# Product-key expert mixer: v tiles of two expert blocks by four feature blocks, and G read four blocks at a time

## The chip, the cores and the metric

The kernel runs on one core of a Trainium2 chip. The metric is the device time of one execution in microseconds (us), the median of several runs. A profiled execution also leaves a trace: for each instruction its engine, its start and its duration, and for idle time before an instruction what released it. The engines are TensorE (PE in the rows; its weight loads are PEld), VectorE (DVE), ScalarE (ACT), GpSimd (POOL) and SyncE (SP, which here only issues transfers).

## What is computed

Two layers of an encoder trunk work on 576 tokens (64 of a running stream and 512 of a new one). Each layer has a token mixer (gated linear attention beside a state-space branch) and then an expert mixer of 16384 experts. Only the expert mixer matters here. Cut to its core:

```python
def one_block(xb):                       # some tokens
    q = (xb @ wq).reshape(n, 8, 256)
    s1, s2 = scores of both halves of q against keys1, keys2      # 128 sub-keys each
    ...                                  # top 16 of each, top 16 of their sums: eidx, gsm = softmax
    u_sel = u_tab[eidx]
    v_sel = v_tab[eidx]
    act = jnp.einsum('td,thkd->thk', xb, u_sel)
    w = gsm * jax.nn.gelu(act, approximate=False)
    return jnp.einsum('thk,thkd->td', w, v_sel)
```

The result, scaled by a modulation vector, is added to the residual, and a norm over the features follows.

## The kernel before

For 448 of the 576 tokens (TD) the expert mixer isn't computed by looking experts up but densely: the weights of all 16384 experts are multiplied. With experts in 128 blocks (EB) of 128, the activations gelu(u x) of one block are a tile of 128 experts by 448 tokens; G, the softmax weights scattered to the same layout (zero where an expert isn't chosen), is multiplied in; and v of the block, 128 experts by 1024 features (8 feature blocks), is multiplied from the left and summed over all blocks. The other 128 tokens (GT) take the way of the reference: 128 rows of u for each token are gathered, one row per token at a time, then 128 rows of v (`gather_u`, `gather_v`; one gather is an indirect transfer issued by GpSimd, its product and sum are one VectorE instruction into `hold`, which lies in two banks of PSUM). At the end the gathered sum is copied to SBUF and transposed by TensorE in eight pieces.

Matrix products are kept near fp32 by splitting each operand in a high and a low part (fp32r): high by a copy on ScalarE, low by a subtraction on GpSimd (for weights) or VectorE (for the expert weights `wh`, `wl`), and three products, high x high, high x low, low x high. So each block of 128x128 costs three matmuls of 448 columns.

The expert mixer runs in this order in `peer()`. First TensorE computes the activations of blocks 0 to 61 (AH) while VectorE does the top-k and G is built; the activations go to DRAM (`a_dram`) and G too (`g_dram`, 7 groups of 64 tokens; in a row of it, 64 tokens of block 0, then of block 1, and so on). Then comes `dense()`, the stage that the change is about. Before, it goes through a list of items, `v_plan`: item i is one feature block d and the expert blocks b0 to b1. An item has eight expert blocks, except for the first seven, which have 1 to 7, and the last eight, which have 8 to 1. For every item one tile of v is loaded (up to 512 KB; the run in DRAM is 128 features, 512 bytes), split, and used for 3 x 8 matmuls into one sum. Sums take turns in the first half of the PSUM tile `work` and a bank of the pool `pa` (four banks, which are also used for the activations `u` and the copies `w`). VectorE then adds the sum to `acc` in SBUF (the first time it copies).

Each step of the list also makes the weights of one block, LW = 2 steps ahead: `weight(b)` reads G for the block (`load_g`, two blocks in a tile, three tiles), reads the stored activation (`load_a`) and copies it to a bank of PSUM on ScalarE, or, for blocks 62 and up, has TensorE compute it just before (`u_mm`, 24 matmuls, then gelu in place). Three further instructions are put on a list and taken from it by `stage()` between the matmuls: the product with G on VectorE (`mul`), the high part on ScalarE (`high`) and the low part on VectorE (`low`).

All instructions of an engine run in the order in which the program issues them. The order on the queues therefore follows the text of the loop. Weight tiles pass through the class `Weights`: raw loads on SP's queue into three buffers (two more in this stage), up to five tiles ahead of the splits; splits two tiles ahead of use. `W.get` issues them. The gathers are driven by the loop itself: every `yield` of `dense()` adds to a counter, and when it passes one the next step of the gathers is issued, so that 264 steps fit in the stage; 259 are used, the last with the transposes. The expert weights have GB + LW = 10 buffers for each part.

Towards the end `residual(d)` reads the residual of a feature block and adds it on VectorE, and `combine(d)` adds a last sum to it, scaled by the modulation. With the last sum of a feature block come the squares for the norm: a square on ScalarE, an add on VectorE (`SumSq.more`), and a product with a matrix of ones on TensorE (`SumSq.mm`), which for blocks 6 and 7 is issued in between.

Of the kernel before, what the change touches and what calls it, by code (L numbers as in the profile page):

```python
# [9 lines left out]
F32 = mybir.dt.float32  # L10
# [8 lines left out]
P = 128  # L19
# [10 lines left out]
EB = 128  # L30
# [3 lines left out]
TG = 64  # L34
NG = TD // TG
GB = 8
LW = 2
AH = 62
RU = 1.7
GC = 0.55  # L40
G0 = 4
# [138 lines left out]
def hybrid_kernel(ctx, tc, A, O):  # L180
# [16 lines left out]
    def pat(name):  # L197
        return pa.tile([P, 512], F32, name=name, tag="pa")
# [880 lines left out]
    def v_plan():  # L1079

        out = [(d, 0, d) for d in range(1, GB)]
        out += [(n % GB, n, n + GB) for n in range(EB - GB)]
        return out + [(d, EB - GB + d, EB) for d in range(GB)]

    def peer(l, h2, h2t, nxt, pq):
        hh, hl = h2
# [3 lines left out]
        ub, vb = {}, {}  # L1092
        for i in range(AH):
            ub[i] = W.add([A["uT"][l, i]])
        for i, (d, b0, b1) in enumerate(plan):
            if AH <= i + LW < EB:
                ub[i + LW] = W.add([A["uT"][l, i + LW]])
            vb[i] = W.add([A["v"][l, b0:b1, :, d * P:(d + 1) * P].rearrange("b e c -> e b c")], vpl, "v")
        W.stop = vb[0]
        if l + 1 < L:  # L1100
            add_mixer(l + 1)
# [48 lines left out]
        def gather_v():  # L1150
            AC.activation(act, act, AF.Gelu)
            DV.tensor_mul(gw, gw, act)
            for j in range(P):
                g = gp.tile([P, D], F32, name=f"gv{j}", tag="g")
                PO.indirect_dma_start(out=g, out_offset=None, in_=A["v"].rearrange("l b e d -> (l b e) d"),  # L1155
                                      in_offset=bass.IndirectOffsetOnAxis(ap=gidx[:, j:j + 1], axis=0))
                if j >= 3:
                    vadd(j - 3)
                gts[j] = g
                yield 1  # L1160
            for j in range(P - 3, P):
                vadd(j)
            yield 1
            xg = gp.tile([P, KB, GT], F32, name="xg", tag="g")
            nc.sync.dma_start(xg, xs_dram[:, :, TD:T])
            gacc = gp.tile([P, D], F32, name="gacc", tag="g")
            AC.activation(gacc, hold, AF.Copy)
            yield 1
            for i in range(2):
                ps = pat(f"gt{l}_{i}")  # L1170
                for b in range(4):
                    PE.transpose(ps[:, b * P:(b + 1) * P], gacc[:, (4 * i + b) * P:(4 * i + b + 1) * P], ident)
                for b in range(4):
# [258 lines left out]

        def load_g(b):

            if b % 2 == 0 and b < EB:
                t_ = dp.tile([P, NG, 2 * TG], F32, name=f"gt{b}", tag="gt", bufs=3)
                nc.sync.dma_start(
                    t_, g_dram[l].rearrange("g p c -> p g c")[:, :, b * TG:(b + 2) * TG])
                gtile[b] = gtile[b + 1] = t_

        def load_a(b):
            if b < AH:
# [5 lines left out]

        def weight(b):

            load_g(b + 4)
            load_a(b + 3)
            if b < AH:
                ps = pat(f"w{l}_{b}")
                AC.activation(ps[:, :TD], ag.pop(b), AF.Copy)
            else:
                ps = ups.pop(b)
                AC.activation(ps[:, :TD], ps[:, :TD], AF.Gelu)  # L1458
            wh = dp.tile([P, TD], F32R, name=f"wh{b}", tag="wh", bufs=GB + LW)
            wl = dp.tile([P, TD], F32R, name=f"wl{b}", tag="wl", bufs=GB + LW)  # L1460

            def mul():
                pv = ps[:, :TD].rearrange("p (g t) -> p g t", t=TG)
                o = b % 2 * TG
                DV.tensor_tensor(pv, pv, gtile.pop(b)[:, :, o:o + TG], op=ALU.mult)

            def high():
                AC.activation(wh, ps[:, :TD], AF.Copy)

            def low():  # L1470
                DV.tensor_tensor(wl, ps[:, :TD], wh.bitcast(F32), op=ALU.subtract)  # L1471
                ws[b] = (wh, wl)

            stages.extend([mul, high, low])

        def stage(n=1):
            for _ in range(n):
                if stages:
                    stages.pop(0)()

        def dense():

            for b in (0, 2):
                load_g(b)
            for b in range(3):
                load_a(b)
            for b in range(LW):
                weight(b)
                stage(3)
            first = set()  # L1490
            for i, (d, b0, b1) in enumerate(plan):
                b = i + LW
                if AH <= b < EB:
                    for _ in u_mm(b):
                        yield 6 * RU
                    yield 6 * RU
                if b < EB:
                    weight(b)
                if b0 == EB - GB:
                    for _ in gat:  # L1500
                        pass
                vh, vl = W.get(vb[i])
                ps = (pat(f"vo{l}_{i}") if i % 2 else work[:, 0, :])[:, :TD]
                n = b1 - b0
                for k in range(n):
                    wh, wl = ws[b0 + k]
                    ds_ = slice(k * P, (k + 1) * P)
                    for j, (vv_, ww) in enumerate(((vh, wh), (vh, wl), (vl, wh))):
                        PE.matmul(ps, vv_[:, ds_], ww, start=k == 0 and j == 0, stop=k == n - 1 and j == 2)  # L1509
                    if k % 2 == 1 and k < n - 1:  # L1510
                        stage()
                        yield 6
                stage(3)
                if b0 >= EB - 2 * GB:
                    combine(d, ps, b1 == EB)
                elif d not in first:
                    first.add(d)
                    DV.tensor_copy(acc[:, d, :TD], ps)
                else:
                    DV.tensor_tensor(acc[:, d, :TD], acc[:, d, :TD], ps, op=ALU.add)  # L1520
                if EB - 3 * GB <= b0 < EB - 2 * GB:
                    residual(d)
                yield 6

        ga2 = m[:, 40:48, :]
        sq_ = []

# [8 lines left out]
        def combine(b, ps, last):  # L1536
# [2 lines left out]
                                        op0=ALU.mult, op1=ALU.add)  # L1539
            if last:  # L1540
                if not sq_:
                    sq_.append(SumSq(dp, 3, f"xo{l}", "gt", 3))
# [137 lines left out]
```

## Time and profile before

| | us |
|---|---|
| median of 3 runs | 5200.94 (5195.92 to 5211.62) |
| the profiled execution | 5198.86 |
| its span in the trace | 5197.1 |

| engine | busy us | share of the span |
|---|---|---|
| TensorE | 4945.4 | 95% |
| VectorE | 3227.8 | 62% |
| GpSimd | 2898.7 | 56% |
| ScalarE | 1962.7 | 38% |

The mean granted clock of TensorE is 0.977 of full speed. The stage `dense()` lies at about 1680 to 2650 us for layer 0 and 4220 to 5180 us for layer 1, some 37% of the span. In it the transfers are at their densest: 295 to 340 GB/s, against a mean of 180.

The busy time of an engine is what its instructions took; a matmul is pipelined, so that one of 448 columns is shown with 0.36 us although the next begins 0.2 us later. A row of the timeline has the start, the duration, the engine, the line, the operation with its output and inputs, and in brackets how long the engine sat idle before and what released it. A row of the chain of work has the start, the duration and what ran.

### The profile page before, as it was taken

The page shows a single profiled execution, that of the slowest core. Times are in us where ns is not written, and L with a number is a line of the kernel's source. Part 1 is how long each engine was busy: PE and PEld are TensorE (multiplying, and loading weights), DVE is VectorE, ACT ScalarE, POOL GpSimd, SP SyncE. Part 2 cuts the span into 40 slices and gives each one's busy share as a digit, 9 for nine tenths or more (in the row PEclk, how much of TensorE's full clock was granted, in tenths as well). Part 3 has the DMA queues.
Part 4 walks back from the last instruction along what each step waited for, and adds up shares of the span by engine and source line. Part 5 has one row for each costly group of instructions (what it writes and reads, how often), then busy time and mean ns, then how long its engine had stood idle before and what let it go on. Part 6 is the DMA issues. An engine that isn't in the chain of part 4 may idle for free.

```text
span 5197.1 us, 77582 instructions
## 1 busy us (share of the span) xinstructions
PE 4945.4 (95%) x29892; PEld 4558.6 (88%) x29892; DVE 3227.8 (62%) x6513; ACT 1962.7 (38%) x3020; POOL 2898.7 (56%) x1986
## 2 busy tenths in 40 slices
PE   8988999989998999999989889998999999999998
PEld 6977888879888999999889878998998889999997
DVE  4687631359997665555646886414799956655564
ACT  3333332233377443223233332423234854332232
POOL 3356543334444777877743555533344557777875
PEclk9999999999999999999999999999999999999999
DMA  3211246523446998888822111232243589988894
GB/s 141 70 58 53 74 139 203 168 95 109 144 153 229 335 338 296 295 297 302 274 78 70 62 50 54 78 100 96 66 146 123 214 271 340 315 297 297 298 310 157
DMA packets 594897, 934.64 MB, mean 180 GB/s; under 512 B 29889, under 2 KB 443073, under 8 KB 591073
## 3 DMA queue, kind: packets, MB, share of 16 engines
q1 hardware_dynamic: 498032, 563.70, 35.5%
q0 software_dynamic: 73728, 268.47, 13.8%
q10 hardware_dynamic: 22768, 97.52, 4.7%
q8 instruction: 237, 3.88, 0.3%
q14 instruction: 132, 1.07, 0.1%
HBM read 826.53 MB, written 103.04 MB: 179 GB/s over the span
## 4 chain that ended last, share of the span: by engine, by line
PE 57%; DVE 20%; issue 9%; POOL 8%; ACT 4%; DMA 2%; ACTq 0%; POOLq 0%; DVEq 0%; SPq 0%
PE pj L476 23%; PE vo L1509 9%; PE work L1509 9%; PE u L1117 8%; POOL wlo L111 3%; DVE tix L1229 2%; POOL gv L1155 2%; DVE cv L635 2%; DVE tv L1228 2%; DVE teq L1304 1%; DVE teid L1312 1%; DVE teq L1309 1%; DVE ob L1394 1%; ACT stg L1369 1%; DVE s L1231 1%
## 5 line engine op out<-in xcount | busy, mean ns | idle before, releaser
L111 POOL TENSOR_TENSOR wlo<-raw,whi 128x1024 fp32r<-128x1024 f32 (+1 forms) x510 | 1265.4, 2482 | 1640.6 <-ACT whi L110 1606.2
L111 POOL TENSOR_TENSOR vlo<-raw,vhi 128x1024 fp32r<-128x1024 f32 (+3 forms) x270 | 620.9, 2300 | 359.8 <-ACT vhi L110 355.9
L110 ACT ACTIVATE whi<-raw 128x1024 fp32r<-128x1024 f32 (+1 forms) x510 | 538.7, 1056 | 219.1 <-issue 149.3
L1117 PE MATMUL u<-n_0hi,whi 128*128 128x448 f32 x1024 | 383.6, 375 | 9.1 <-DVE tsc L1293 7.0
L1117 PE MATMUL u<-n_1hi,whi 128*128 128x448 f32 x1024 | 383.0, 374 | 9.1 <-DVE tsc L1293 7.0
L1509 PE MATMUL work<-wh,vhi 128*128 128x448 f32 x1024 | 376.2, 367 | 14.0 <-ACT vhi L110 14.0
L1117 PE MATMUL u<-n_0hi,wlo 128*128 128x448 f32 x1024 | 377.9, 369 | 3.5 <-POOL wlo L111 3.5
L1117 PE MATMUL u<-n_1hi,wlo 128*128 128x448 f32 x1024 | 377.7, 369 | 3.3 <-POOL wlo L111 3.3
L1458 ACT ACTIVATE u<-u 128x448 f32<-128x448 f32 x132 | 69.7, 528 | 816.3 <-PE u L1117 806.3
L1117 PE MATMUL u<-n_0lo,whi 128*128 128x448 f32 x1024 | 377.7, 369 | 0.0
L1117 PE MATMUL u<-n_1lo,whi 128*128 128x448 f32 x1024 | 377.2, 368 | 0.0
L1509 PE MATMUL vo<-wh,vlo 128*128 128x448 f32 x1024 | 374.9, 366 | 0.7 <-POOL vlo L111 0.7
L1509 PE MATMUL vo<-wh,vhi 128*128 128x448 f32 x1024 | 375.0, 366 | 0.3 <-DVE wl L1471 0.3
L1509 PE MATMUL work<-wl,vhi 128*128 128x448 f32 x1024 | 375.2, 366 | 0.0
L1509 PE MATMUL work<-wh,vlo 128*128 128x448 f32 x1024 | 374.9, 366 | 0.0
L1509 PE MATMUL vo<-wl,vhi 128*128 128x448 f32 x1024 | 374.8, 366 | 0.0
L1184 DVE SCALAR_TENSOR_TENSOR hold<-gv,gw,hold 128x1024 f32<-128x1024 f32 x254 | 326.4, 1285 | 54.6 <-DMA gv<-in_v,gidx 51.8
L110 ACT ACTIVATE vhi<-raw 128x1024 fp32r<-128x1024 f32 (+3 forms) x270 | 271.8, 1008 | 136.4 <-issue 94.3
L1148 DVE SCALAR_TENSOR_TENSOR gu<-gu,hold 128x1024 f32<-128x1024 f32 x256 | 307.5, 1213 | 16.2 <-DMA gu<-in_u,gidx 16.0
L1394 DVE TENSOR_SCALAR ob<-work,sT 128x128 f32<-128x128 f32 x896 | 295.5, 401 | 0.7 <-PE gb L1368 0.6
L476 PE MATMUL pj<-n_0hi,whi 128*128 128x288 f32 x1248 | 285.6, 311 | 1.4 <-ACT whi L110 1.4
L476 PE MATMUL pj<-n_1hi,whi 128*128 128x288 f32 x1248 | 283.3, 309 | 0.1
(526 smaller groups left out, 12648.9 us busy)
## 6 DMA issues: line engine op xcount, KB each, us to landing
raw<-in_wblk SPq DMA_DIRECT2D x256, 512.0 KB
raw<-in_uT SPq DMA_DIRECT2D x256, 512.0 KB
raw<-in_v SPq DMA_DIRECT2D x242, 512.0 KB
gt<-g_dram SPq DMA_DIRECT2D x128, 448.0 KB
adaw<-in_w_ada SPq DMA_DIRECT2D x96, 512.0 KB
g_dram<-stg ACTq DMA_DIRECT2D x12, 4096.0 KB
a_dram<-ag ACTq DMA_DIRECT2D x124, 224.0 KB
ar<-a_dram SPq DMA_DIRECT2D x124, 224.0 KB
```

The costliest lines, as they stand in the source:

```text
L110: self.nc.scalar.activation(hi, r, AF.Copy)
L111: self.nc.gpsimd.tensor_tensor(lo, r, hi.bitcast(F32), op=ALU.subtract)
L476: PE.matmul(ps[:mcols, a, :HT], w[:, ws], xx[:, k, H2[a]], start=k == 0 and j == 0, stop=k == nk - 1 and j == 2)
L635: DV.scalar_tensor_tensor(c, ext[:, i:i + N], w[:, 4 * cb + i:4 * cb + i + 1], c, op0=ALU.mult, op1=ALU.add)
L1117: PE.matmul(ps[:, :TD], w[:, ws], x[:, k, :TD], start=k == 0 and j == 0, stop=k == KB - 1 and j == 2)
L1148: DV.scalar_tensor_tensor(g, g, 1.0, hold, op0=ALU.mult, op1=ALU.mult, accum_out=act[:, j:j + 1])
L1155: PO.indirect_dma_start(out=g, out_offset=None, in_=A["v"].rearrange("l b e d -> (l b e) d"), in_offset=bass.IndirectOffsetOnAxis(ap=gidx[ ...
L1184: DV.scalar_tensor_tensor(hold, g, gw[:, j:j + 1], hold, op0=ALU.mult, op1=ALU.add)
L1228: DV.max(v[:n, ti, b, js], sb_)
L1229: DV.max_index(ix[:n, ti, b, js], v[:n, ti, b, js], sb_)
L1394: DV.tensor_scalar(ob[:, j, :], iotp, sT[:, 1, tk:tk + 1], sT[:, 2, tk:tk + 1], op0=ALU.is_equal, op1=ALU.mult)
L1509: PE.matmul(ps, vv_[:, ds_], ww, start=k == 0 and j == 0, stop=k == n - 1 and j == 2)
```

## The change

A v tile now holds two expert blocks by four feature blocks (the run in DRAM is 512 features, 2 KB), always 512 KB, so 128 tiles for a layer. Features are in two halves, h = 0 and 1. One tile gives 24 matmuls: six into each of four sums, which lie in the two halves of `work` and in two banks of `pa` that are held for the stage. A sum runs over eight expert blocks, four tiles, then four sums are evicted, and the other half of the features takes the banks. The half h = 1 begins with a short sum over blocks 0 to 3 and ends with one over 124 to 127, so that the halves are offset by four blocks.

LW goes from 2 to 4, and before the loop the four weights are issued before the first of their further steps, of which six are taken there. The expert weights have 8 buffers instead of 10. G is read for four blocks at once (runs of 1 KB, 896 KB a tile), two tiles instead of three. The residual steps are taken one at a time at the beginning of a tile's matmuls, behind `weight(b)`. The transposes of the gathered sum write to `hold2`, the PSUM tile that held it, instead of banks of `pa`. The squares at the end have two buffers instead of three.

```diff
-LW = 2
+LW = 4
+VB = 8
+QF = 4
@@ v_plan
-        out = [(d, 0, d) for d in range(1, GB)]
-        out += [(n % GB, n, n + GB) for n in range(EB - GB)]
-        return out + [(d, EB - GB + d, EB) for d in range(GB)]
+        sums = [(1, 0, GB // 2)]
+        for c in range(0, EB, GB):
+            sums += [(0, c, c + GB), (1, c + GB // 2, min(c + GB // 2 + GB, EB))]
+        return [(h, c, c == c0, c + 2 == c1) for h, c0, c1 in sums for c in range(c0, c1, 2)]
@@ peer
-            vb[i] = W.add([A["v"][l, b0:b1, :, d * P:(d + 1) * P].rearrange("b e c -> e b c")], vpl, "v")
+            vb[i] = W.add([A["v"][l, c:c + 2, :, h * QF * P:(h + 1) * QF * P].rearrange("b e c -> e b c")], vpl, "v")
@@ gather_v
-                ps = pat(f"gt{l}_{i}")
+                ps = hold2[:, i, :]
@@ load_g
-            if b % 2 == 0 and b < EB:
-                t_ = dp.tile([P, NG, 2 * TG], F32, name=f"gt{b}", tag="gt", bufs=3)
+            if b % 4 == 0 and b < EB:
+                t_ = dp.tile([P, NG, 4 * TG], F32, name=f"gt{b}", tag="gt", bufs=2)
...
@@ weight
-            load_g(b + 4)
+            load_g(b + 3)
...
-            wh = dp.tile([P, TD], F32R, name=f"wh{b}", tag="wh", bufs=GB + LW)
+            wh = dp.tile([P, TD], F32R, name=f"wh{b}", tag="wh", bufs=VB)
@@ dense
-            for b in (0, 2):
-                load_g(b)
+            load_g(0)
             for b in range(3):
                 load_a(b)
             for b in range(LW):
                 weight(b)
-                stage(3)
+            stage(6)
...
                 if b < EB:
                     weight(b)
-                if b0 == EB - GB:
+                if res:
+                    residual(res.pop(0))
+                if h == 0 and c == EB - GB:
                     for _ in gat:
                         pass
                 vh, vl = W.get(vb[i])
-                ps = (pat(f"vo{l}_{i}") if i % 2 else work[:, 0, :])[:, :TD]
...
+                for q in range(QF):
+                    d, ps = h * QF + q, accs[q]
+                    for k in range(2):
+                        wh, wl = ws[c + k]
+                        ds_ = slice((k * QF + q) * P, (k * QF + q + 1) * P)
+                        for j, (vv_, ww) in enumerate(((vh, wh), (vh, wl), (vl, wh))):
+                            PE.matmul(ps, vv_[:, ds_], ww, start=begin and k == 0 and j == 0,
+                                      stop=end and k == 1 and j == 2)
+                    stage(3 if q == QF - 1 else 1)
+                    if end:
+                        done = c + 2
+                        if done > (EB - 2 * GB if h == 0 else EB - 3 * GB // 2):
+                            combine(d, ps, done == EB)
...
+                        if done == (EB - 2 * GB if h == 0 else EB - 3 * GB // 2):
+                            res.append(d)
+                    yield 6
+        accs = [work[:, i, :TD] for i in range(2)] + [pat(f"va{l}_{i}")[:, :TD] for i in range(2)]
...
-        whole = sum(3 * (b1 - b0) + 24 * RU * (AH <= i + LW < EB) for i, (d, b0, b1) in enumerate(plan)
-                    if b0 < EB - GB - 2)
+        whole = sum(24 + 24 * RU * (AH <= i + LW < EB) for i in range(len(plan) - 6 - 2))
```

## Rows read from the trace of the kernel before

**Rows 1.** Stretches of 100 us: busy time by engine, PEclk, DMA share, GB/s

```profile
1700.00:1800.00 100.00, 100.00 (x495) 92.67 (x494) 62.36 (x109) 43.06 (x65) 75.18 (x47) 1.00 1.11 339
2300.00:2400.00 100.00, 100.00 (x496) 92.66 (x495) 56.89 (x63) 31.20 (x44) 78.00 (x52) 1.00 0.87 295
```

**Rows 2.** Chain of work in order of time: start, us, what; the ninth item, both layers

```profile
1711.67 4.87 PE work L1509 x24
4251.40 4.86 PE work L1509 x24
```

**Rows 3.** TensorE's waits, 1680 to 2650 us: us in total, times, longest

```profile
PE work L1509 <- ACT vhi L110: 7.1, 2, 6.9
```

**Rows 4.** Timeline at the beginning of dense(): start, duration, engine, line, operation

```profile
1685.99 0.74 PE L1509 MATMUL work<-wh,vhi 128*128 128x448 f32 x1 [6.89 <-ACT vhi L110]
...
4225.41 0.74 PE L1509 MATMUL work<-wh,vhi 128*128 128x448 f32 x1 [6.88 <-ACT vhi L110]
...
4226.32 0.58 PE L1509 MATMUL work<-wh,vlo 128*128 128x448 f32 x1
4226.69 0.58 PE L1509 MATMUL vo<-wh,vhi 128*128 128x448 f32 x1
...
1681.71 0.55 ACT L1455 ACTIVATE w<-ar 128x448 f32<-128x448 f32 x1 [0.60 <-DMA ar<-a_dram]
...
1685.64 1.02 ACT L110 ACTIVATE vhi<-raw 128x128 fp32r<-128x128 f32 x3
...
1703.09 1.04 ACT L110 ACTIVATE vhi<-raw 128x1024 fp32r<-128x1024 f32 x1
...
1683.54 0.62 DVE L1471 TENSOR_TENSOR wl<-w,wh 128x448 fp32r<-128x448 f32 x1 [0.61 <-ACT wh L1468]
...
1704.21 2.42 POOL L111 TENSOR_TENSOR vlo<-raw,vhi 128x1024 fp32r<-128x1024 f32 x1 [2.29 <-ACT vhi L110]
...
1673.78 0.37 SPq L100 DMA_DIRECT2D raw<-in_v  x1
1674.37 0.97 SPq L1437 DMA_DIRECT2D gt<-g_dram  x2
```

**Rows 5.** Stretches of 1 us at the same place, columns as in rows 1

```profile
1679.00:1680.00 1.00, 0.10 (x1) 0.00 (x0) 0.00 (x0) 0.55 (x1) 0.00 (x0) 1.00 1.14 362
...
1681.00:1682.00 1.00, 0.00 (x0) 0.00 (x0) 0.00 (x0) 0.40 (x2) 0.00 (x0) 0.60 1.07 357
...
1691.00:1692.00 1.00, 1.00 (x5) 0.91 (x4) 0.00 (x0) 1.00 (x3) 0.36 (x1) 0.78 1.04 308
```

**Rows 6.** Timeline at the end of the stage, layer 0, VectorE and TensorE

```profile
2637.41 0.81 DVE L1538 SCALAR_TENSOR_TENSOR acc<-vo,mod,acc 128x64 f32<-128x64 f32 x2
...
2639.70 0.80 DVE L1538 SCALAR_TENSOR_TENSOR acc<-work,mod,acc 128x64 f32<-128x64 f32 x2
...
2642.22 1.21 PE L281 MATMUL xo<-xo0q,ones 128*128 128x288 f32 x4 [1.81 <-DVE xo0q L267]
...
2645.71 1.24 PE L281 MATMUL xo<-xo0q,ones 128*128 128x288 f32 x4 [0.70 <-ACT xo0q L260]
```

**Rows 7.** Timeline: the last gather and the transposes of its sum, both layers

```profile
2573.42 0.95 POOL L1155 DMA_INDIRECT gv<-in_v,gidx  x1 [0.16 <-DVE hold L1184]
...
2584.06 1.97 PE L1172 MATMUL gt<-ident,gacc 128*128 128x128 f32 x8 [4.16 <-ACT gacc L1167]
...
5110.31 0.95 POOL L1155 DMA_INDIRECT gv<-in_v,gidx  x1 [0.16 <-issue]
...
5120.63 1.09 PE L1172 MATMUL gt<-ident,gacc 128*128 128x128 f32 x8 [1.00 <-ACT gacc L1167]
```

**Rows 8.** Timeline of VectorE in mid-stage: an eviction, a product with G, a gather product

```profile
1813.85 0.62 DVE L1520 TENSOR_TENSOR acc<-acc,work 128x448 f32<-128x448 f32 x1 [1.85 <-PE work L1509]
1814.39 0.63 DVE L1465 TENSOR_TENSOR w<-w,gt 128x448 f32<-128x448 f32 x1
1814.93 1.21 DVE L1148 SCALAR_TENSOR_TENSOR gu<-gu,hold 128x1024 f32<-128x1024 f32 x1
```

More of the change, by code (lines that the diff above doesn't have):

```diff
@@ L1094, in peer @@
             ub[i] = W.add([A["uT"][l, i]])
-        for i, (d, b0, b1) in enumerate(plan):
+        for i, (h, c, _, _) in enumerate(plan):
             if AH <= i + LW < EB:
                 ub[i + LW] = W.add([A["uT"][l, i + LW]])
-            vb[i] = W.add([A["v"][l, b0:b1, :, d * P:(d + 1) * P].rearrange("b e c -> e b c")], vpl, "v")
+            vb[i] = W.add([A["v"][l, c:c + 2, :, h * QF * P:(h + 1) * QF * P].rearrange("b e c -> e b c")], vpl, "v")
         W.stop = vb[0]
@@ L1433, in load_g @@
         def load_g(b):
-            if b % 2 == 0 and b < EB:
-                t_ = dp.tile([P, NG, 2 * TG], F32, name=f"gt{b}", tag="gt", bufs=3)
+            if b % 4 == 0 and b < EB:
+                t_ = dp.tile([P, NG, 4 * TG], F32, name=f"gt{b}", tag="gt", bufs=2)
                 nc.sync.dma_start(
-                    t_, g_dram[l].rearrange("g p c -> p g c")[:, :, b * TG:(b + 2) * TG])
-                gtile[b] = gtile[b + 1] = t_
+                    t_, g_dram[l].rearrange("g p c -> p g c")[:, :, b * TG:(b + 4) * TG])
+                for i in range(4):
+                    gtile[b + i] = t_
         def load_a(b):
@@ L1458, in weight @@
                 AC.activation(ps[:, :TD], ps[:, :TD], AF.Gelu)
-            wh = dp.tile([P, TD], F32R, name=f"wh{b}", tag="wh", bufs=GB + LW)
-            wl = dp.tile([P, TD], F32R, name=f"wl{b}", tag="wl", bufs=GB + LW)
+            wh = dp.tile([P, TD], F32R, name=f"wh{b}", tag="wh", bufs=VB)
+            wl = dp.tile([P, TD], F32R, name=f"wl{b}", tag="wl", bufs=VB)
             def mul():
                 pv = ps[:, :TD].rearrange("p (g t) -> p g t", t=TG)
-                o = b % 2 * TG
+                o = b % 4 * TG
                 DV.tensor_tensor(pv, pv, gtile.pop(b)[:, :, o:o + TG], op=ALU.mult)
@@ L1488, in dense @@
                 weight(b)
-                stage(3)
-            first = set()
-            for i, (d, b0, b1) in enumerate(plan):
+            stage(6)
+            seen = set()
+            for i, (h, c, begin, end) in enumerate(plan):
                 b = i + LW
@@ L1502, in dense @@
                 vh, vl = W.get(vb[i])
-                ps = (pat(f"vo{l}_{i}") if i % 2 else work[:, 0, :])[:, :TD]
[L1504 to L1523, printed above, removed]
+                for q in range(QF):
[11 more added lines that the diff above has]
+                            combine(d, ps, done == EB)
+                        elif d not in seen:
+                            seen.add(d)
+                            DV.tensor_copy(acc[:, d, :TD], ps)
+                        else:
+                            DV.tensor_tensor(acc[:, d, :TD], acc[:, d, :TD], ps, op=ALU.add)
+                        if done == (EB - 2 * GB if h == 0 else EB - 3 * GB // 2):
+                            res.append(d)
+                    yield 6
+        res = []
+        accs = [work[:, i, :TD] for i in range(2)] + [pat(f"va{l}_{i}")[:, :TD] for i in range(2)]
         ga2 = m[:, 40:48, :]
@@ L1541, in combine @@
                 if not sq_:
-                    sq_.append(SumSq(dp, 3, f"xo{l}", "gt", 3))
+                    sq_.append(SumSq(dp, 3, f"xo{l}", "gt", 2))
                 if b >= 6:
```

## The prediction

> **What bounds the kernel now.** The change touches only the last stage of each layer's expert mixer, dense() and the gathers woven into it. I read the stretches of that stage first. From about 1700 to 2570 us (layer 0) and 4250 to 5110 us (layer 1) TensorE is busy for 100.00 of every 100 us at granted clock 1.00 [rows 1]; the reader is to see that VectorE (57 to 62%) and GpSimd (75 to 78%) are not full, and that the DMA share falls from 1.11 to 0.87 when the stored activations stop, while TensorE does not change. Next the chain in order of time: an item of 24 matmuls takes 4.87 us, 0.203 us each [rows 2]. The number of such matmuls is the same before and after: 1024 blocks x 3 for v and 66 x 24 for u, in each layer. So a faster transfer in mid-stage buys nothing, and the change can win or lose only where TensorE waits: at the stage's beginning (6.9 us before the first v matmul), at the transposes of the gathered sum (4.2 and 1.0 us) and in the last few us [rows 3, 4, 6, 7]. The waits in rows 4, 6 and 7 add up to 20.7 us over both layers, some 23 with the end of layer 1 like that of layer 0, 0.44% of the time; no gain can pass that unless a matmul itself gets cheaper, and no row shows why it should.
>
> **The beginning of the stage.** Before, the first v tiles are short (1, 2, 3 expert blocks), so the loads ahead are 64, 128 and 192 KB, the first three splits on ScalarE take 1.02 us together, and the first low part is small [rows 4]. After, each tile is 512 KB. Let t0 be the start of the first w copy, 1681.71 us in layer 0; it waits for the first stored activation [rows 4].
> - The third raw load is issued at 1673.78, right ahead of the G and activation reads [rows 4]. It grows by 320 KB; at 362 GB/s [rows 5] that is 0.9 us more in front of that activation. The two G tiles of 448 KB become one of 896 KB, the same bytes. Longer rows may give back a part, so between 0 and 0.9 us: I take t0 + 0.5.
> - LW = 4 puts four w copies (0.55 us each) ahead of everything else on ScalarE. The fourth needs three more reads of 224 KB, 1.9 us at 360 GB/s, so they end at t0 + 2.5. The split of two weights goes back and forth between ScalarE and VectorE (0.6 us a step [rows 4]): wh of block 0 to 3.0, wl 3.7, product of block 1 to 4.3, wh of block 1 to 4.9.
> - Then the loop begins with weight(4), whose copy stands on ScalarE ahead of the v splits. Its activation is read behind the next G tile: 896 + 224 KB after t0 + 1.9, 3.2 us, so t0 + 5.1; the copy ends at 5.7 (between 5.5 and 6.5). Queued behind it are three v splits of 1.04 us [rows 4]; TensorE waits for the first: 6.8 us, against 4.28 before (1685.99 less 1681.71).
> - The third matmul needs the low part: 2.42 us on GpSimd [rows 4], so the matmuls flow from t0 + 9.2, 1691.4 us with t0 moved by 0.5.
> - The clock: it was granted 0.60 in 1681 to 1682, and 0.78 in 1691 to 1692, between them the lower level (1.2 GHz), back to 1.00 about 5.5 us after the first v matmul [rows 5]. There a matmul starts every 0.37 us [rows 4]. The same 5.5 us from 1691.4 on give 15 matmuls by 1696.9, and 2 came before.
> - Before, 108 matmuls (items of 1 to 8 blocks) were done at 1711.67 [rows 2]. After: 17 + (1711.67 - 1696.9) / 0.203 = 90. The loss is 18 matmuls, 3.7 us. In layer 1 with 4225.41 for 1685.99 and 4251.40 for 1711.67 [rows 2, 4] it is 16.5 matmuls, 3.3 us. **Together +7.0 us**; bounds +2 (t0 not moved, the w copy not last, the clock back sooner) and +11 (a second late transfer).
> The Trainium skill, DMA: Bandwidth & Descriptors, section Specifications, puts the least transfer for line rate at 512 B, which the rows of the old v tiles already have; by it longer rows would give nothing back, t0 would move by the full 0.9 us and the sum would be 0.8 us higher. The DMA share of 1.07 to 1.14 at 357 to 362 GB/s [rows 5] is with 512 B rows and speaks for it.
>
> **Mid-stage.** Loads, splits (128 full tiles for 135, the same bytes) and evictions (132 for 135) stay hidden under TensorE's 4.87 us for a tile. G reads go from 64 to 32 on SP's queue. What is new is the reuse of a sum. Before, two banks take turns and an eviction has a whole item of 24 matmuls. After, four sums end in one tile, each is evicted when its six matmuls are through, and its bank is needed 18 matmuls, 3.65 us, later (42 matmuls where a u block stands between). On VectorE such a tile has four evictions and two weight steps of 0.62 and one or two gather products of 1.21 [rows 8], 5 to 6 us of work spread over 4.87 + 3.65 us; the first eviction ends some 2 us into the tile, the last 1.5 us after it, each 2 us or more ahead of its bank's reuse. The eviction of the old kernel starts 0.25 us after its matmuls where VectorE is idle [rows 8]. Cost 0; if VectorE is late by more, see the first rival. Two banks are left for u and w where there were four (one of them lent to every second sum): a u bank is free again after the block's last weight step in the same tile, one tile ahead of need.
>
> **The gathers.** The pace constant divides by 5410 instead of 5568 weighted matmuls, so gathers come 2.9% faster: 3.16 instead of 3.07 in a tile with u. TensorE stalls at the transposes because from the last gather's place to theirs there are 48 matmuls, 9.73 us, while the chain (gather, three sums, copy) took 10.64 and 10.3 us, and began late by 3.3 and 0.4 us [rows 7]. The places are again 48 matmuls apart. The residual steps, in which VectorE waits for a transfer, now stand behind the load of the u block rather than behind that of v, so I expect the late start of layer 0 to shrink: 1.5 us of stall in each layer, **-2 us together** (bounds -5.2, both gone, and +4, both as late as 3.3 + 1 with combines in between).
>
> **The end.** Combine, square and add of one feature block take 2.29 us in turn between VectorE and ScalarE [rows 6]. Before, the last sums end 9, 6 and 3 matmuls apart, and the flush of squares before the last three matmuls waits 1.81 us for the chain [rows 6]. After, feature blocks 4 to 7 end 1.22 us apart: block 4 starts in the chain 3.4 us before the nominal end (3 x 1.22 less 0.25), so after two turns of 2.29 the flush begins 1.4 us behind it; then come 1.2 us of flush, six matmuls instead of three, the last combine, square and sum: 7.0 us from the nominal last matmul to the last sum, against 5.9 before (2642.22 - 1.81 + 0.6 = 2641.0 to 2646.95 [rows 6]). **+1.0 us in each layer** (0 to 1.5).
>
> **Sum.** +7.0 - 2.0 + 2.0 = +7 us against the profiled execution, 5198.9 us (span 5197.1 and 1.8 us around it), so 5206. That execution lay 2.1 us under the median of the three runs, so 5208.
>
> **Rivals.**
> - *Late evictions (slower).* VectorE is in order, and in the v-only part it holds gather products that can wait for a transfer. If it is more than 2 us behind at the ends of sums, TensorE stands still at each. The price: 15 sums end in that part of a layer, 30 in all; one gather product of 1.21 us too late at each is 36 us, 5244 us, and the clock may fall in the pauses. It decides from 3.65 us between an eviction's matmuls and its end. Against it speaks the 0.25 us [rows 8].
> - *The loads ahead pay (no loss, or faster).* Three full tiles lie ready (1.5 MB for 0.4), the activations behind them arrive sooner and the beginning costs nothing; with the gather stall gone it gives -3 us or so, 5198. A gain over 15.6 us would need two thirds of all 23 us of waits.
> - *The sums cycle through banks.* If TensorE pauses a little between groups of six in four banks and the clock falls, a matmul costs 0.37 instead of 0.203 us [rows 2, 4]; over a tenth of the two stages (1850 us) that is some 80 us, 5290. Rows 1 show 1.00 with a change of bank at every 24. The Trainium skill, TensorE: Matmul & The Clock Gate, section "A second HAM failure mode: psum-queue depth-cycling", tells of a kernel that lost throughput in this way.
> - *It does not do what it says where it counts:* longer rows lower the DMA share, and no engine gets faster. This is inside the forecast.
>
> **How the numbers follow.** Forecast with its bounds 0.77; late evictions 0.12, mostly over the bound; loads that pay 0.08, half of it within the bound; bank cycling 0.03. A measurement of this kernel tells about 0.3%, 15.6 us, from no change. Faster by more 0.04; within 0.78; slower by more 0.18 (0.11 + 0.03 + 0.04 from the upper end of the forecast). The forecast's own range: +7 with the bounds of its parts taken together gives about -3 to +16, with the spread of the runs 5194 to 5220; with the smaller cases of late evictions 5194 to 5225.
>
> **What would show it.** The first v matmul about 7.3 us after the old t0 instead of 4.28, behind a w copy and a full split, and a wait on the low part after it; 108 matmuls done 3 to 4 us later; mid-stage slices still 100.00 at clock 1.00, with a lower DMA share in the v-only part; transposes waiting 0 to 3 us; the flush of squares waiting longer. Wrong would be waits of TensorE on VectorE at the ends of sums, a mid-stage slice under 99, or a matmul that isn't 0.203 us.

## The result

| | before | after |
|---|---|---|
| device time, median | 5200.2 us | 5336.1 us |
| ratio, 95% interval | | 1.0257 (1.0238 to 1.0277) |
| profiled execution / its span | 5198.9 / 5197.1 us | 5330.8 / 5328.8 us |
| packets of the queue that SP fills / MB / share | 498032 / 563.70 / 35.5% | 242832 / 563.70 / 33.4% |

The changed kernel is slower by 2.6%, some 135 us, where 8 us were forecast and 5225 us was the upper end. The longer rows did halve the packets. TensorE lost time in another place. Stretches of 100 us of the changed kernel, columns as in [rows 1]:

```profile
1700.00:1800.00 100.00, 97.14 (x472) 88.01 (x471) 59.38 (x103) 39.17 (x60) 67.52 (x42) 1.00 0.92 322
2300.00:2400.00 100.00, 97.86 (x481) 89.73 (x480) 58.81 (x65) 28.64 (x40) 78.36 (x53) 1.00 0.87 303
2500.00:2600.00 100.00, 86.70 (x413) 79.47 (x412) 53.54 (x66) 25.15 (x34) 65.63 (x44) 0.93 0.78 266
```

Against [rows 1] TensorE's 100.00 has become 96 to 99 in mid-stage, with 472 and 481 matmuls in 100 us for 495 and 496. The granted clock is 1.00 in all but one of the stretches from 1700 to 2500 us (0.98 from 2100 to 2200 us); from 2500 us on it falls further. TensorE's waits in layer 0 of the changed kernel (us in total, times, longest), to be read against [rows 3]:

```profile
PE work L1514 <- DVE acc L1525: 34.3, 27, 12.6
PE work L1514 <- DVE acc L1545: 14.0, 4, 11.3
PE work L1514 <- ACT vhi L112: 10.6, 1, 10.6
PE work L1514 <- DVE acc L1523: 1.4, 2, 0.7
PE work L1514 <- POOL vlo L113: 1.3, 1, 1.3
PE hold L1175 <- DVE acc L1178: 1.3, 1, 1.3
```

Lines 1523, 1525 and 1545 are the three ways in which a sum leaves its bank. The layer has 33 sets of four sums, and there are 27 + 4 + 2 = 33 waits: one at the end of each set. Layer 1 has the same (34.4, 14.1 and 1.4 us); the two layers make 99.6 us. One such end, as pieces of the chain in order of time, and in the timeline:

```profile
1737.73 1.25 PE work L1514 x6
1738.98 0.02 issue
1739.00 0.63 DVE acc L1525
1739.63 0.04 issue
1739.68 1.50 PE work L1514 x6
1741.18 2.48 PE va L1514 x12
```

```profile
1739.00 0.62 DVE L1525 TENSOR_TENSOR acc<-acc,work 128x448 f32<-128x448 f32 x1 [2.53 <-PE work L1514]
1739.68 0.47 PE L1514 MATMUL work<-wh,vhi 128*128 128x448 f32 x1 [0.71 <-DVE acc L1525]
```

Six matmuls into one half of the tile `work` end; VectorE, idle for 2.53 us, evicts that half at once; TensorE waits for it, and only then come the six matmuls into the other half, which nothing has to be evicted from. Those six take 1.50 us instead of 1.22. So a stop costs 0.71 + 0.28 us even with VectorE ready and waiting. Of the 66 stops 58 are of this kind: 0.7 to 0.9 us each, 42.5 us together, with the eviction begun within 0.25 us of the last matmul. At the other eight, 57.1 us, VectorE is late: four are of 11.3 to 13.0 us and four of 1.0 to 3.3 us.

Where the time went, by the n-th matmul of the stage (all matmuls counted from the first v matmul, in the timelines of before and after; the time of the n-th after less that before):

| part of the stage | layer 0 | layer 1 |
|---|---|---|
| up to the 108th matmul, with what lies ahead of the stage | +2.8 us | +1.5 us (64.2 from 62.7) |
| 108th to 4000th | +32.4 | +35.0 |
| 4000th to 4400th (the residual steps) | +25.4 | +29.2 |
| 4400th to the last, the 4676th (with the squares) | +2.0 | +3.4 |

They add up to 131.7 us, by which the spans differ. The second line is the short stops, in the main: the 27 waits of layer 0 on line 1525 without the longest are 26 in 21.7 us, two of them with a late VectorE (1.6 and 3.0 us); with 0.28 us each for the slow restart, 29.0 us; a slower pace of some matmuls, told of below, adds 2.2. The third line is two long waits, 12.6 and 11.3 us. Around the first of them (timeline):

```profile
2548.40 0.38 SPq L102 DMA_DIRECT2D raw<-in_v  x1
2548.83 0.46 SPq L1440 DMA_DIRECT2D gt<-g_dram  x1
2549.35 0.55 SPq L1538 DMA_DIRECT2D xb<-xs_dram  x1
2558.94 0.82 DVE L1540 SCALAR_TENSOR_TENSOR acc<-acc,mod,xb 128x64 f32<-128x64 f32 x2 [10.34 <-DMA xb<-xs_dram]
2560.20 0.61 DVE L1525 TENSOR_TENSOR acc<-acc,work 128x448 f32<-128x448 f32 x1
2560.87 0.74 PE L1514 MATMUL work<-wh,vhi 128*128 128x448 f32 x1 [12.59 <-DVE acc L1525]
```

The residual's load xb is issued behind a v tile of 512 KB and the new G tile of 896 KB and lands 9.6 us later. VectorE stands at the residual step for 10.34 us, the product and the eviction stand behind it, and TensorE behind the eviction. The same in small, in mid-stage, behind a gather of u (two rows of the timeline, and the 10 us that follow, columns as in [rows 1]):

```profile
2183.89 1.22 DVE L1151 SCALAR_TENSOR_TENSOR gu<-gu,hold 128x1024 f32<-128x1024 f32 x1 [3.39 <-DMA gu<-in_u,gidx]
...
2188.65 0.74 PE L1514 MATMUL work<-wh,vhi 128*128 128x448 f32 x1 [2.97 <-DVE acc L1525]
```

```profile
2190.00:2200.00 10.00, 10.00 (x47) 9.22 (x46) 5.52 (x7) 1.20 (x2) 6.11 (x5) 0.92 0.97 343
```

VectorE waits 3.39 us for the gathered rows, the eviction is late, TensorE stops for 2.97 us, and the granted clock behind the stop is 0.92. Layer 1 has such a stop of 3.26 us, and each layer one more, of 1.6 and 1.0 us.

### The profile page after: what moved, and what is told of

The parts are those of the page before. It is cut to its first block, busy times and chain, and to the rows that moved or that the text cites. A ratio compares the mean times of both kernels' runs of the same rounds, so it can differ in the third digit from the quotient of the medians.

```text
span 5328.8 us, 77248 instructions
## 1 busy us (share of the span) xinstructions
PE 4976.1 (93%) x29892; PEld 4562.3 (86%) x29892; DVE 3224.3 (61%) x6507; ACT 1953.6 (37%) x3006; POOL 2894.9 (54%) x1972
## 3 DMA queue, kind: packets, MB, share of 16 engines
q1 hardware_dynamic: 242832, 563.70, 33.4%
## 4 chain that ended last, share of the span: by engine, by line
PE 64%; DVE 20%; issue 5%; POOL 4%; ACT 4%; DMA 2%; ACTq 0%; SPq 0%; DVEq 0%; POOLq 0%
PE pj L478 22%; PE work L1514 11%; PE u L1120 11%; PE va L1514 11%; DVE tix L1232 2%; POOL wlo L113 2%; DVE cv L637 2%; DVE tv L1231 2%; DVE teq L1307 1%; DVE teid L1315 1%; DVE teq L1312 1%; DVE ob L1397 1%; ACT stg L1372 1%; DVE s L1234 1%; PE gb L1371 1%
## 5 line engine op out<-in xcount | busy, mean ns | idle before, releaser
L113 POOL TENSOR_TENSOR vlo<-raw,vhi 128x1024 fp32r<-128x1024 f32 x256 | 615.1, 2404 | 458.2 <-ACT vhi L112 441.3
L112 ACT ACTIVATE vhi<-raw 128x1024 fp32r<-128x1024 f32 x256 | 269.8, 1055 | 323.3 <-issue 298.9
L1514 PE MATMUL va<-wh,vhi 128*128 128x448 f32 x1024 | 377.9, 369 | 0.0
L1514 PE MATMUL va<-wl,vhi 128*128 128x448 f32 x1024 | 377.0, 368 | 0.0
L1514 PE MATMUL va<-wh,vlo 128*128 128x448 f32 x1024 | 376.4, 368 | 0.0
L1514 PEld LDWEIGHTS work<-wh,vhi 128*128 128x128 f32 x1024 | 194.7, 190 | 161.3 <-DVE acc L1525 89.1
L1469 DVE TENSOR_TENSOR u<-u,gt 128x448 f32<-128x448 f32 x132 | 83.3, 631 | 335.5 <-ACT u L1462 325.3
```

The costliest lines, as they stand in the source:

```text
L112: self.nc.scalar.activation(hi, r, AF.Copy)
L113: self.nc.gpsimd.tensor_tensor(lo, r, hi.bitcast(F32), op=ALU.subtract)
L1514: PE.matmul(ps, vv_[:, ds_], ww, start=begin and k == 0 and j == 0, stop=end and k == 1 and j == 2)
```

## The experiments

Theory A: the two halves of `work` are one tile, and the waits go by the tile, so a matmul into one half waits for the eviction of the other. Theory B, the prediction's first rival: evictions come late, and a bank's own reuse waits. Theory C, its third: filling four banks in turn slows TensorE.

| kernel | median us | ratio to before (interval) | slow-paced matmuls of some 4600, layer 0 / 1 |
|---|---|---|---|
| after | 5336.1 | 1.0257 (1.0238, 1.0277) | 540 / 972 |
| sums interleaved | 5287.8 | 1.0162 (1.0121, 1.0204) | 1074 / 2022 |
| evictions later | 5271.3 | 1.0132 (1.0088, 1.0176) | 3576 / 510 |
| xb ahead | 5291.3 | 1.0171 (1.0129, 1.0212) | 1008 / 1008 |
| interleaved, xb ahead | 5236.2 | 1.0068 (1.0047, 1.0088) | 546 / 3492 |
| the same, v split early | 5252.4 | 1.0092 (1.0058, 1.0126) | 852 / 1344 |
| before, sums in two halves | 5344.9 | 1.0260 (1.0220, 1.0299) | 792 / 654 |
| four mendings | 5239.2 | 1.0060 (1.0036, 1.0083) | 282 / 3486 |
| the same, G two at a time | 5237.2 | 1.0055 (1.0036, 1.0073) | 3954 / 564 |
| three mendings | 5218.0 | 1.0044 (1.0031, 1.0057) | 588 / 3198 |
| the same, lead of three | 5205.0 | 1.0011 (0.9998, 1.0024) | 462 / 402 |
| the same, halves as a pair inside | 5212.1 | 1.0024 (1.0007, 1.0042) | 4278 / 4248 |

The last column counts, in the profiled execution, matmuls in groups of six that ran at 0.2067 instead of 0.2027 us each (by the starts in the timeline, the groups without a stop). Each ratio is against executions of the kernel before in the same session; their medians lie between 5193.6 and 5203.6 us, so versions of different sessions are to be compared by their ratios.

**Sums interleaved.**

```diff
-accs = [work[:, i, :TD] for i in range(2)] + [pat(f"va{l}_{i}")[:, :TD] for i in range(2)]
+va = [pat(f"va{l}_{i}")[:, :TD] for i in range(2)]
+accs = [work[:, 0, :TD], va[0], work[:, 1, :TD], va[1]]
```

> The two halves of the tile `work` are no longer used one behind the other: the order of the four sums is work half 0, va_0, work half 1, va_1. Theory A (the two halves count as one tile, so the six matmuls into half 1 wait for VectorE to have read half 0): the eviction of half 0 gets six matmuls, 1.2 us, of cover; the 31 or so short waits of 0.7 to 0.9 us in each layer go, 25 us a layer, and the two long ones of 11 to 13 us in each layer get 1.2 us shorter: 5336 - 55 = about 5280. Theory B (VectorE is late with the evictions as such, so that a bank's own reuse waits): nothing of that changes, 5336. Theory C (four banks filled in turn slow TensorE down): 5336 as well.

5287.8 us. TensorE's waits on evictions in layer 0:

```profile
PE work L1514 <- DVE acc L1525: 15.5, 6, 11.6
PE work L1514 <- DVE acc L1546: 12.8, 2, 12.0
```

Of 33 waits 8 are left, two of them the long ones. With the same four banks, the same evictions and the same work on VectorE, 25 stops are gone because six matmuls into another tile stand between the halves. That is A; B and C expected nothing.

**Evictions one group later.** Each sum is evicted behind the next group's six matmuls, the last two together.

```diff
-if end:
+for d, ps in ([(h * QF + q - 1, accs[q - 1])] * (q > 0) + [(d, ps)] * (q == QF - 1)) if end else []:
```

> Order of the sums as in the changed kernel, but the eviction of each sum is issued one group of six matmuls later (the last two together), so no matmul of the same tile follows an eviction of the other half of `work`, except in the next tile. Theory A: the short waits go as in the interleaved kernel, though every eviction is later; the long waits in the residual stretch fall by up to 2.4 us: about 5275. Theory B: later evictions make the reuse wait longer, 5340 to 5380. Theory C: 5336.

5271.3 us. A later eviction is better, which B rules out. The waits of layer 0:

```profile
PE work L1514 <- ACT vhi L112: 17.7, 2, 10.4
PE hold L1175 <- ACT gacc L1170: 10.5, 1, 10.5
PE work L1514 <- DVE acc L1525: 2.2, 4, 0.6
```

The long waits at sums are gone as well, but VectorE still waits for xb, and the delay comes out at a v split ahead of the transposes (7.3 of the 17.7 us; the other 10.4 are the stage's beginning) and at the transposes (10.5).

**The residual's load ahead.** In the changed kernel, each xb is loaded in the tile in which its sum ends, one to four tiles before its use.

```diff
+load_x(d)
 res.append(d)
...
-t_ = dp.tile([P, TD], F32, name=f"xb{b}", tag="ag", bufs=4)
-nc.sync.dma_start(t_, xs_dram[:, b, :TD])
+t_ = xbs.pop(b)
```

> Only the loads of the residual are moved: each is issued in the tile in which its sum ended, one to four tiles ahead of the residual steps that use it; the residual steps stay at the tile's start. Theory A with the residual as amplifier: VectorE no longer waits 9 to 10 us for the load at the two tiles where a sum ends, so the waits of 12.6 and 11.3 us in each layer fall to under 1 us, 45 us together, with some us for the clock that fell in them: 5336 - 50 = about 5286; the short waits stay, 27 or so a layer. Rival (the long waits have another cause, the gathers or the raw loads): 5330 to 5340.

5291.3 us, 45 less. The waits of layer 0; line 1551 is combine, 1545 in the changed kernel:

```profile
PE work L1514 <- DVE acc L1525: 22.5, 27, 3.3
PE work L1514 <- DVE acc L1551: 3.6, 4, 0.9
```

All stops are still there, and the longest is 3.3 us: the load made the two long ones out of ordinary ones. The 3.3 us are the stop behind the gather. At the transposes TensorE now waits 5.0 us, for 1.3 in the changed kernel.

**Both.**

> Sums in the order work half 0, va_0, work half 1, va_1, and the residual's loads ahead. If the two causes are all there is beside the stage's beginning and end (about +11 us) and some matmuls at 0.207 us (about 5 us): 5336 - 55 - 50 less what is shared = 5215 (5205 to 5230). If something else in the change costs (full v tiles, four G blocks at a time, two banks less for u and w), it stays above 5240.

5236.2 us: 48 + 45 us of the two alone should give 5243, so they do not overlap. But some 35 us over the kernel before stayed, above the range expected. At a sum's end the chain now shows this:

```profile
1734.29 0.62 DVE acc L1525
1734.91 1.14 DVE gu L1151 x2
1736.05 0.54 DVE wl L1475
1736.58 0.54 DVE acc L1525
1737.25 1.45 PE work L1514 x6
```

Here the first rival is seen by itself, in small: two gather products and a weight step stand between two evictions, and TensorE waits, 6 times and 4.1 us in layer 0.

**The first v blocks split early**, added to both: fetched and split after two w copies instead of five.

```diff
-for b in range(LW):
+for b in range(2):
     weight(b)
+got = W.get(vb[0])
+for b in range(2, LW):
+    weight(b)
```

> Sums interleaved and the residual's loads ahead as in the kernel with both (5236 us), and the first v blocks are fetched and split behind the second w copy instead of behind the fifth. Theory (the beginning's cost is the order on ScalarE: five w copies ahead of the first v split): TensorE's wait for the first high part falls from 10.4 to about 6.5 us in each layer, 8 us together: 5228. Rival (the bytes of three full v tiles ahead of the activations cost it, so the order doesn't matter): 5236. Uncertain by some 10 us, because stretches of matmuls at 0.207 us come and go from run to run.

5252.4 us: not faster. The theory of ScalarE's order falls. TensorE's first wait only changes its cause (8.7 us for wh instead of 10.4 for vhi), and the activation read now stands on SP behind the v tiles. The kernel with four mendings, below, has the same beginning; its chain there:

```profile
1693.26 10.19 DMA ar<-a_dram
...
1706.73 1.49 PE work L1519 x3
```

A read of 224 KB takes 10.19 us from issue, and TensorE stands 4.86 us at the first sum's end. From the first v matmul to the 54th, the two profiles with this order lose 6 to 7 us in each layer against the kernel before; with the change's own order, in the kernels with both and with three mendings, it is 0.8 to 1.3 us. The chain points to the bytes ahead of the activations, of which this order puts more there; no run moves them alone.

**The kernel before with its two sums in the two halves of `work`**, nothing else changed.

```diff
-ps = (pat(f"vo{l}_{i}") if i % 2 else work[:, 0, :])[:, :TD]
+ps = work[:, i % 2, :TD]
```

> The kernel before with one line changed: its two sums that take turns lie in the two halves of the tile `work`, where one of them had a tile of its own. Nothing of the change itself is in it. Theory A (two halves of one PSUM tile count as one for the waits): TensorE stops at each of the 264 ends of items until VectorE has read the other half, 0.8 to 1.2 us each: 5200 + 264 x 1.0 = 5465 (5410 to 5520). Theory B (late evictions, or the new order of sums, or four banks in turn): a bank is reused as before, 5200.

5344.9 us: one line makes the old kernel as slow as the changed one. The size was over-estimated, since I counted all 264 ends: where a u block stands between two items its 24 matmuls cover the eviction. The chain, and two stretches of 100 us:

```profile
1734.32 5.11 PE work L1509 x24
1739.45 0.63 DVE acc L1520
1740.22 5.21 PE work L1509 x24
```

```profile
1700.00:1800.00 100.00, 85.75 (x400) 73.88 (x401) 50.83 (x89) 35.37 (x52) 59.15 (x37) 1.00 0.87 277
2300.00:2400.00 100.00, 100.00 (x495) 92.70 (x494) 57.91 (x62) 28.84 (x40) 79.87 (x54) 1.00 0.88 298
```

From one item to the next it is 5.9 us instead of 4.87 [rows 2], and with u blocks between, 100.00 again. No v tile, order of sums or G tile of the change is in this kernel. Theory A is shown. By the trace it is the end of VectorE's eviction that releases TensorE; whether a program must have this wait between two banks of one tile is not tested.

**Four mendings**: evictions later, xb ahead, early v split, and the transposes of both halves of hold2 ahead of VectorE's reading of the first (they had the same wait, 1.3 us).

> The changed kernel with four mendings: each eviction issued one group of six matmuls later, the residual's loads ahead, the first v split behind the second w copy, and the transposes of both halves of hold2 ahead of VectorE's reading of the first. If stalls of TensorE, and the slower pace of 0.207 us that follows some of them, are all that the change cost, what is left is the order of the end: 5200 (5190 to 5215), level with the kernel before or a little faster. If the full v tiles or the four G blocks cost anything by themselves, it stays over 5220.

**The same with G two blocks at a time** (`load_g`, and the buffers of the squares, as before).

> The same with G read back two expert blocks at a time, as in the kernel before (64 reads of 448 KB in place of 32 of 896 KB). By the prediction the size of the G reads is worth nothing, as they lie under TensorE's work: within 10 us of the kernel with all mendings. If the larger G reads help (fewer issues on SP's queue) it is slower by more; if they hurt (the raw loads behind them come late) it is faster by more.

5239.2 and 5237.2 us. The first is far above the 5200 expected, and the size of the G reads is not the reason: undone, it changes nothing. What was left had to be the beginning, which the early split had made worse, and the pace (3768 matmuls at 0.004 us, 15 us, in the profile of the first).

**Three mendings**: without the early split.

> The changed kernel with three of the four mendings: evictions one group of six matmuls later, the residual's loads ahead, both transposes ahead of VectorE's reading; the beginning of the stage is left as the change has it. Theory (the other order at the beginning cost 7.5 us in each layer up to the 54th v matmul, by the two profiles with it): 5239 - 15 = 5224, and 5205 to 5210 in an execution whose long stretches run at 0.203 us a matmul. Rival (the beginning is no matter): 5239.

**The same with three weights made ahead** (LW = 3).

> The same with three weights in place of four made ahead of the v tiles, so one w copy and one activation less stands before the first v split. Theory (the beginning is set by the copies queued on ScalarE and the activations behind them): TensorE's wait falls by a further 2 to 3 us in each layer, 5219; rival (with a lead of three the weights of a tile come late in mid-stage, and TensorE waits on wh or wl): over 5235.

5218.0 and 5205.0 us. Without the early split the ratio falls from 1.0060 to 1.0044, some 8 us, though the two intervals overlap; in the profiles the 108th matmul comes 5.4 and 6.2 us sooner after the last u matmul ahead of the stage. A lead of three takes 13 us more, in the same session. In its profile TensorE's first wait falls from 10.4 to 8.9 us in each layer, and the waits at the transposes from 3.1 and 1.3 us to 0.2 us and none, some 7 us together; the rest is open, and as a copy and a load go at once, this run does not tell them apart. With it the changed kernel is level with the kernel before (interval 0.9998 to 1.0024), with all the change's v tiles and G tiles in it.

**The pace.** Every profile of a changed kernel has stretches in which a matmul takes 0.2067 us, at granted clock 1.00. The chain of the kernel with three mendings, left and right of a stop in layer 1:

```profile
4446.17 2.43 PE va L1516 x12
4448.60 2.45 PE work L1516 x12
...
4454.04 2.71 PE work L1516 x12
4456.75 2.48 PE va L1516 x12
```

12 matmuls took 2.43 us before the stop and 2.48 after it; it stays so to 5110 us, 3198 matmuls, 0.004 us each, 12.8 us. For this the kernel before was profiled again.

> The kernel before, unchanged, for a second profile of it. Open is whether the pace of 0.207 us a matmul, which every profile of a changed kernel shows in some stretches and the first profile of the kernel before in none, belongs to the new order of sums. If it does: 0.203 throughout again. If it is drawn anew at each stall of TensorE, whatever the kernel: it may stand in a stretch here too, the likelier the more stalls, and this kernel has few (some 4 in a stage), so a stretch without it says little and one with it decides.

It took 5197.6 us. Two stretches of 20 us in layer 1:

```profile
5060.00:5080.00 20.00, 20.00 (x101) 18.53 (x100) 14.67 (x16) 6.51 (x10) 14.74 (x10) 1.00 0.86 292
5090.00:5110.00 20.00, 20.00 (x99) 18.16 (x98) 15.47 (x19) 7.18 (x11) 18.50 (x13) 1.00 0.96 331
```

101 and 99 matmuls: after a matmul that came 0.3 us late at 5089 us, 174 matmuls ran at the slower pace, until the stop at the transposes ended it. So it does not belong to the change; it can change at a stop, and the change made many.

**The halves as a pair inside**, evicted together behind the third group:

```diff
+accs = [va[0], work[:, 0, :TD], work[:, 1, :TD], va[1]]
...
+for d, ps in [(h * QF + p, accs[p]) for p in ((0,), (), (1, 2), (3,))[q]] if end else []:
```

> As the kernel with a lead of three, but with the two halves of `work` as the second and third of the four sums, evicted together behind the third group of six; va_0 and va_1 are evicted behind their own groups. Each half is then needed again 12 matmuls, 2.4 us, after its eviction is issued, and no group of the same tile follows. Theory (the four stalls of 0.5 us that are left in each layer come from the eviction of half 1, issued only six matmuls ahead of the reuse): they go, 8 x 0.8 = 6 us, and with fewer stalls fewer stretches at 0.207 us: 5205 - 6 to - 12 = 5193 to 5199, level with the kernel before. Rival (VectorE's queue, with two gather products ahead of an eviction, is the cause wherever the eviction stands): 5205.

The four stops of 0.5 us in each layer are gone, as the theory said: no wait on line 1527 is left in either layer (one of 0.7 us at a combine has come in each). Yet the time is 5212.1 us, by the ratio no faster than the lead of three. The profiled execution took 5222.7, and its chain reads so throughout:

```profile
1895.86 2.48 PE work L1516 x12
```

From 1689 to 2566 and from 4239 to 5116 us the pace is 0.2067: with no stop in between, the pace in which the stage began held to the transposes. 8526 matmuls at 0.004 us are 34 us; the fastest execution of this kernel, 5189.7, is 33 us faster than the profiled one. That the fastest ran at 0.203 throughout is argued from this, not seen.

## Why the prediction was wrong

**The step that failed is mid-stage at cost 0.** I asked when each bank is written again, 18 matmuls after its eviction, and found 2 us of cover. For the banks by themselves that was right at 58 of the 66 ends: VectorE began the eviction within 0.25 us of the last matmul (0.02 us in the end shown). What the runs showed in place of 0 is 66 stops with 99.6 us of waits, 32 and 35 us of loss in the two layers' mid-stage alone. The wait was on another bank: the two sums called `work` are halves of one tile, and TensorE was made to wait for the tile, six matmuls after the first half and not 18. That six matmuls later the other half comes is read from the order of accs; that the halves share a tile stands in the kernel before, where only one half was a sum. The Trainium skill, Perfetto Trace Analysis, section Matmuls, has independent groups of matmuls rotate through different PSUM banks so that the eviction of one lies under the next; the changed kernel does this, and the trace shows a stop at every set of sums, until the neighbours in time were different tiles as well.

**The first rival** had the place right (waits of TensorE on VectorE at the ends of sums) and the reason for a part of them. A late VectorE was behind eight stops: four with a gather, as it says (8.8 us), and four with the residual's load, which it does not name (48.2 us). At the other 58, with 42.5 us, VectorE was in time, and TensorE stopped all the same. So its price was wrong: it counted 30 ends of 1.2 us, and there were 66 with 99.6 us. In the kernel with both mendings its own mechanism was seen, at 4.1 us in layer 0.

**The gathers' step** put the residual steps "behind the load of the u block" and took this for an advantage. The raw load of the v tile and the 896 KB G read also went ahead of xb: VectorE's longest wait for it in layer 0 rose from 5.88 to 10.34 us. This is the second step that failed: it cost 45 us, as the kernel with xb ahead shows. In the kernel before the residual step came behind the eviction, not ahead of it. The transposes lost most of their wait (1.3 us between the halves in each layer, for 4.2 and 1.0), so the -2 us were there, but, as it seems, by luck: TensorE's two long stops, 24 us, lay just ahead, and in the kernel with three mendings, which has neither, the transposes wait 3.1 and 1.3 us. And 55 us of the change lie in this stretch.

**The beginning** came out near the steps. The first v matmul came 7.02 us after the first w copy and the low part held the third for 1.32 us; the flow began at 9.45 us (forecast 6.8 and 9.2, and 0.5 for a later copy):

```profile
1680.94 2.25 ACT L1459 ACTIVATE w<-ar 128x448 f32<-128x448 f32 x4 [1.57 <-DMA ar<-a_dram]
1686.38 0.55 ACT L1459 ACTIVATE w<-ar 128x448 f32<-128x448 f32 x1 [0.89 <-DMA ar<-a_dram]
1686.87 2.93 ACT L112 ACTIVATE vhi<-raw 128x1024 fp32r<-128x1024 f32 x3
1687.96 0.74 PE L1514 MATMUL work<-wh,vhi 128*128 128x448 f32 x1 [10.60 <-ACT vhi L112]
1690.39 0.74 PE L1514 MATMUL work<-wh,vlo 128*128 128x448 f32 x1 [1.32 <-POOL vlo L113]
```

The three splits stand behind a fifth w copy that waits for its activation, as told. The loss at the 108th matmul, from the end of the u matmuls ahead of it, was 4.5 us in layer 0 (2.8, and the u matmuls ended 1.7 sooner) and 4.3 in layer 1 (64.2 less 59.9), for 3.7 and 3.3 forecast.

**The end** was +2.0 and +3.4 us instead of +1.0: it has three of the stops too, of 0.9 us each, and the flush of squares waited 1.23 us, not longer than before. In the kernel with three mendings the same matmuls give -1.0 and +1.3 us.

**The third rival** named a fall of the clock. At 1700 to 2100 us the granted clock was 1.00 with a stop at every set of sums; after the waits of 3 us and more it did fall (0.92 behind the one of 2.97 us, 0.93 from 2500 to 2600 us). By the section that the prediction cites from the Trainium skill, TensorE: Matmul & The Clock Gate, short pauses between groups in cycling banks cost one kernel clock; no stretch of short stops here shows that.

With the two causes mended, a lead of three, and the transposes in order, the kernel takes 5205 us, level with the kernel before; with the change's own lead of four the ratio is 1.0044, some 23 us, of which the slower pace makes 15 in the profile. So the rest of the sum, beginning, gathers and end, was about the right size; what it lacked were these two causes. One slip in it changes nothing: the waits of rows 4, 6 and 7 add up to 21.4 us, not 20.7 (the 0.70 us of rows 6 is left out). No version here beats the kernel before.

## What to carry to other kernels

Before two sums are made neighbours in time, ask not only which bank each lies in, but which tile: two banks of one tile are one thing for the waits, and an eviction of one stops the matmuls into the other, however idle the evicting engine is. Put another tile's group between them, or evict both behind the second. A load that an in-order engine will wait for should be issued where its need is known, not where it is used: behind two large transfers, 224 KB took 10 us.

## What the runs showed of the hardware

The pace of matmuls of this shape is one of two, 0.2027 or 0.2067 us, both at granted clock 1.00. It changes at a stop of TensorE or at the transposes, and holds as long as none comes, up to 877 us here; of 302 stretches of 30 and more matmuls without a visible stop, in all profiles, 4 show a change of pace. Of the 136 stops in the profiles of after and of the kernel with xb ahead that have six undisturbed matmuls on both sides, those out of the faster pace led to the slower 24 times in 105, and those out of the slower back to the faster 23 times in 31. It is no plain draw: in the kernel before with its sums in two halves, where the stops are much alike, 120 of 135 change the pace, one way and back in turn. What decides it stays open. It is worth up to 34 us, 0.65%, in this kernel, so kernels that differ by less than that can't be ranked by one profile; it is also the likely reason, though only argued, why executions of one version lie between 5189.7 and 5237.4 us.
